# A two-layer decoder trunk in fp32: raw gate/up weights in six tiles instead of three, and weight preparation by 1,024 columns

## The chip, the core and the metric

The kernel runs on one core of one Trainium2 chip. The metric is the device time in microseconds. TensorE (PE) multiplies, VectorE (DVE), ScalarE (ACT) and GpSimd (POOL) do the elementwise work, and SyncE's queue (SP) issues every DMA of the kernel.

## What is computed

Sequence 1,024, width 1,024, two layers, each an attention and a SwiGLU mixer. Cut to what matters here:

```python
def swiglu(h, w_gate_up, w_down):
    gate, up = jnp.split(h @ w_gate_up, 2, axis=-1)     # 1024 -> 2 x 2816
    return (jax.nn.silu(gate) * up) @ w_down            # 2816 -> 1024
...
    for layer in range(DEPTH):
        h = rms_norm(x, mix_pre_g[layer])
        ...   # layer 0: differential attention; layer 1: stick-breaking attention with
        ...   # q = h @ b_w_q and k, v = rms_norm(x, kv_norm_g) @ kv_w
        x = x + rms_norm(m, mix_post_g[layer])
        f = swiglu(rms_norm(x, ffn_pre_g[layer]), ffn_w_gate_up[layer], ffn_w_down[layer])
        x = x + rms_norm(f, ffn_post_g[layer])
```

## The kernel before, in words

Every fp32 operand of a product is split into a high part (fp32r, a rounded copy) and a low part (what the rounding lost), and a product is three passes on PE: high by high, low by high, high by low. The two mixers' products are cut further into seven half-size products of sums and differences of blocks, in place of eight.

**The order of the work** is made when the kernel is built. `Weaver` (line 82) runs the kernel's parts as threads. A thread names the engine and the planned cost of its next step (`yield DVE(1024)`), takes tiles from pools (`yield acq(S_tr)`) and waits for events; of the ready steps of an engine the one with the lower priority number goes first. `InOrder` (line 277) records each instruction as it comes, so that every engine and SP's queue have one fixed order. On the chip the engines keep that order and wait for each other by semaphores; how long things take there doesn't change it.

**The gate/up stage** (`gate_up`, line 1735, once for each layer; mixer A at about 0.65 to 1.1 ms, mixer B at about 2.02 to 2.45 ms) runs over 22 blocks of 128 hidden columns. A block, called a quad below, is loaded by `loader` into two raw tiles (128x1024, the gate columns and the up columns), with a third raw tile as scratch. `quad` (line 510) makes seven operands from them: five need a sum or a difference on DVE; each is rounded by ACT into a `w` tile's first half, and the low part is subtracted by POOL (six of seven) or DVE (one). There are nine `w` tiles. The three raw tiles are given back when all seven operands of the quad are there. PE then does 7 x 12 = 84 matmuls of 512 columns for the quad (against `hT` or `hx`, the split activations), into one of eight PSUM banks for each operand; `take` (line 1785) adds each bank into four 128x512 tiles (named `e`) on DVE and ACT.

```python
S_raw = Slots(tiles(cpool, 3, [P, 1024], F32, "raw"))
S_tr = Slots(tiles(cpool, 5, [P, 1024], F32, "tr"))
```

For each pair of quads `pair_ops` (line 1747) forms the sums and differences that the down product needs and stores them to HBM (`op`); its three sums take a tile of the 12 scratch tiles `S_sg` or, where none is free, one of the five `tr` tiles. `tr` tiles are otherwise used where the stages change (transpositions, norms, `transition`).

**The preparation of the second attention's weights** (`pre_weights`, line 413) runs beside mixer A. For 24 blocks (b_w_q and kv_w, eight each of q, k, v; a job below) it loads 128x1024 values into a `tr` tile, multiplies by the norm's gain (a column for each of eight 128-column pieces), and stores the high part and the low part to HBM (`prebq`, `prebk`, `prebv`). Eight more jobs without a gain follow for b_w_o (`prewo`). ACT makes the high part by eight 128-column activations, DVE the low part by eight 128-column instructions.

**The down stage** of mixer A follows (about 1.1 to 1.36 ms, `down`), with operands made from `hT` on the same engines, and ends with `transition`, which uses `tr` tiles.

## Time and profile before

| | |
|---|---|
| median of 3 runs | 2686.43 us (2685.59 to 2689.43) |
| the profiled execution | 2685.22 us |
| its span, first to last instruction | 2683.4 us, so 1.8 us lie around it |
| mean granted TensorE clock | 0.977 of full |
| busy: PE, DVE, ACT, POOL | 2519.7, 2061.2, 1288.8, 806.8 us |
| raw gate/up loads | 88 of 512 KB, median 5.1 us from issue to landing |

An engine's busy time is a union of its instructions; a busy PE is not a PE at its peak, and a share over the whole span mixes stages with different limits. The useful views are therefore the table by stage, the waits of one stage, and the chain of work that ended last. In group rows "x144 | 79.4, 590" is the count, the busy us and the mean ns of one. A wait is put down to what came last.

### The profile page before, as it was taken

The numbers are of one execution on the slowest core, as the hardware profiler recorded it, in microseconds if no ns is written. First come the engines' busy times: TensorE is split into PE (matmuls) and PEld (weight loads), VectorE is DVE, ScalarE is ACT, GpSimd is POOL, SyncE is SP. The second block draws the span as 40 slices with busy tenths as digits, with TensorE's granted clock in tenths as the row PEclk, the third lists the DMA queues.
The fourth block names the chain that finished last, engine by engine and source line by source line (L and its number), as shares of the span: only waits on it lengthen the run. The fifth ranks groups of instructions, "written<-read, shape, count | busy, mean of one in ns | idle before, by whom it ended". The sixth has DMA issues, their size and how long they took to land.

```text
span 2683.4 us, 37281 instructions
## 1 busy us (share of the span) xinstructions
PE 2519.7 (94%) x12555; PEld 2117.6 (79%) x12555; DVE 2061.2 (77%) x3559; ACT 1288.8 (48%) x2926; POOL 806.8 (30%) x733
## 2 busy tenths in 40 slices
PE   8999999897999989899899999999989999999998
PEld 8998999775877777677678888888777877777887
DVE  4767676866887878689978888778777777676898
ACT  4555565644444444454246655556454333334532
POOL 2111112333343333435510000000033444445553
PEclk9999999998999999899999999999999999999999
DMA  6333333441566545665474444444543433337325
GB/s 172 82 79 79 91 81 103 120 165 67 171 210 203 198 145 174 234 208 180 170 243 109 112 113 113 120 117 130 199 153 110 130 129 127 98 102 239 110 83 177
DMA packets 286335, 378.78 MB, mean 141 GB/s; under 512 B 24448, under 2 KB 182528, under 8 KB 285568
## 3 DMA queue, kind: packets, MB, share of 16 engines
q1 hardware_dynamic: 286144, 376.40, 45.2%
q8 instruction: 99, 1.62, 0.3%
q14 instruction: 92, 0.75, 0.1%
HBM read 230.70 MB, written 114.16 MB: 129 GB/s over the span
## 4 chain that ended last, share of the span: by engine, by line
PE 42%; DVE 29%; DMA 11%; issue 7%; ACT 5%; POOL 4%; SPq 1%; DVEq 0%; ACTq 0%; POOLq 0%
PE bank L286 42%; DVE e L286 7%; DVE raw L286 7%; DVE tr L286 6%; DMA raw<-in_ffn_w_gate_up_dram 5%; POOL w L286 3%; ACT w L286 2%; DVE rB L286 2%; DMA tr<-in_kv_w_dram 2%; DVE atB L286 1%; DVE w L286 1%; SPq L286 1%; DVE fb L286 1%; ACT e L286 1%; DVE fa L286 1%
## 5 line engine op out<-in xcount | busy, mean ns | idle before, releaser
L286 PE MATMUL bank<-hT,w 128*128 128x512 f32 x3264 | 817.5, 402 | 49.9 <-POOL w L286 21.1
L286 POOL TENSOR_TENSOR w<-raw,w 128x512 fp32r<-128x512 f32 (+1 forms) x363 | 552.9, 1535 | 772.1 <-ACT w L286 698.6
L286 PEld LDWEIGHTS bank<-hT,w 128*128 128x128 f32 x3264 | 611.5, 192 | 192.9 <-POOL w L286 33.0
L286 ACT CAST w<-raw 128x512 fp32r<-128x512 f32 x398 | 244.6, 621 | 603.3 <-DVE raw L286 412.1
L286 PE MATMUL bank<-hx,w 128*128 128x512 f32 x1584 | 367.7, 389 | 4.7 <-DVE hx L286 4.7
L286 DVE TENSOR_TENSOR e<-e,bank 128x512 f32<-128x512 f32 x480 | 311.9, 676 | 68.5 <-ACT e L286 49.1
L286 PEld LDWEIGHTS bank<-hx,w 128*128 128x128 f32 x1584 | 296.9, 188 | 68.4 <-DVE hx L286 7.0
L286 PE MATMUL bank<-w,hT 128*128 128x384 f32 (+1 forms) x1728 | 344.9, 346 | 5.5 <-DMA w<-prewo 3.1
L286 PEld LDWEIGHTS bank<-w,hT 128*128 128x128 f32 x1728 | 300.2, 189 | 15.8 <-DMA w<-prewo 3.5
L286 PE MATMUL bank<-w,fb 128*128 128x512 f32 x1204 | 295.3, 395 | 14.2 <-DVE e L286 5.8
L286 PEld LDWEIGHTS bank<-w,fb 128*128 128x128 f32 x1204 | 227.8, 190 | 66.7 <-DVE fb L286 4.2
L286 DVE TENSOR_TENSOR raw<-raw 128x512 f32<-128x512 f32 x88 | 80.1, 930 | 159.6 <-DMA raw<-in_ffn_w_gate_up_dram 159.6
L286 PE MATMUL bank<-ident,tr 128*128 128x128 f32 x1059 | 161.4, 280 | 37.0 <-DVE tr L286 19.0
L286 PE MATMUL bank<-w,fa 128*128 128x512 f32 x692 | 181.7, 403 | 14.4 <-DVE e L286 4.5
L286 PEld LDWEIGHTS bank<-ident,tr 128*128 128x128 f32 x1059 | 128.0, 143 | 68.0 <-DVE tr L286 20.1
L286 POOL MEMSET atB<- 128x128 f32 x128 | 25.1, 205 | 498.3 <-PE bank L286 492.7
L286 PEld LDWEIGHTS bank<-w,fa 128*128 128x128 f32 x692 | 133.6, 194 | 47.6 <-POOL w L286 4.4
L286 POOL TENSOR_TENSOR sm<-sm,nhalf 128x1 f32<-128x1 f32 (+1 forms) x72 | 56.8, 790 | 299.3 <-DVE sm L286 296.7
L286 DVE TENSOR_TENSOR_SCAN rB<-rB,zeroB 128x512 f32<-128x512 f32 (+3 forms) x145 | 134.8, 947 | 6.0 <-ACT rB L286 5.6
L286 DVE TENSOR_TENSOR raw<-raw,raw 128x512 f32<-128x512 f32 x132 | 134.4, 1018 | 0.0
L286 ACT CAST atB<-bank 128x512 fp32r<-128x512 f32 (+1 forms) x160 | 84.5, 554 | 88.8 <-PE bank L286 82.7
L286 DVE TENSOR_TENSOR atB<-bank,atB 128x512 fp32r<-128x512 f32 (+1 forms) x160 | 97.6, 629 | 32.9 <-ACT atB L286 32.4
(224 smaller groups left out, 3854.5 us busy)
## 6 DMA issues: line engine op xcount, KB each, us to landing
raw<-in_ffn_w_gate_up_dram SPq DMA_DIRECT2D x88, 512.0 KB, 5.1
op<-e SPq DMA_DIRECT2D x99, 256.0 KB, 4.1
xy<-st SPq DMA_DIRECT2D x192, 128.0 KB, 2.3
xyB<-stB SPq DMA_DIRECT2D x176, 128.0 KB, 3.8
fb<-op SPq DMA_DIRECT2D x79, 256.0 KB, 3.5
wd<-in_ffn_w_down_dram SPq DMA_DIRECT2D x36, 512.0 KB, 6.2
hT<-wd SPq DMA_DIRECT2D x72, 256.0 KB, 5.4
raw<-in_a_w_qkv_dram SPq DMA_DIRECT2D x96, 128.0 KB, 2.6
```

What stands on the lines that cost most here:

```text
L286: return tc.keep_in_program_order(f(*a, **k))
```

## The change

Four things change, and the planner then builds a new order from them.

1. When all seven activation operands of a mixer are there, a thread `lend_raw` takes three of the five `tr` tiles and lends them to `loader` as raw tiles (`S_rx`) until the gate/up stage's end. `loader` takes raw tiles from both pools. It does so in both mixers.
2. The three sums of `pair_ops` take `S_sg` tiles only, and `pair_ops` gets priority -5 in place of 25 (A) and 46 (B).
3. `pre_weights` multiplies by the gain with one DVE instruction of 1,024 columns, rounds with one ACT instruction of 1,024 columns, and subtracts with one DVE instruction of 1,024 columns, instead of eight and eight of 128.
4. `pre_weights` waits for the seven activation operands instead of the phase's end and 25 us; its threads' priority is 40 in place of 60, and its planned pause between jobs 6.0 us in place of 13.5. With three `tr` tiles lent, two are left for it.

```diff
--- before.py
+++ after.py
@@ -335,7 +335,7 @@
     actd = {f: drp.tile([P, T], F32, name=f"act{f}") for f in range(ND, NF)}
     opd = [{i: drp.tile([P, 512], F32, name=f"op{p}_{i}") for i in DORD} for p in range(ND // 2)]
 
-    S_half, S_trx = Slots(), Slots()
+    S_half, S_trx, S_rx = Slots(), Slots(), Slots()
 
     def halves(t):
         return [t[:, :512], t[:, 512:]]
@@ -411,8 +411,8 @@
     pres = []
 
     def pre_weights(ready):
-        yield ready
-        yield delay(25.0)
+        for ev in ready:
+            yield ev
 
         def work(job, raw, hi):
             if job.gain is not None:
@@ -420,20 +420,11 @@
                 yield g_ev
             h = hi.t.bitcast(F32R)
             if job.gain is not None:
-                for c in range(NC):
-                    cs = slice(c * P, c * P + P)
-                    yield ACT(P, 1)
-                    act.activation(h[:, cs], raw.t[:, cs], AF.Copy, scale=g[:, c:c + 1])
-                for c in range(NC):
-                    cs = slice(c * P, c * P + P)
-                    yield DVE(P + 58)
-                    dve.scalar_tensor_tensor(raw.t[:, cs], raw.t[:, cs], g[:, c:c + 1], hi.t[:, cs],
-                                             op0=ALU.mult, op1=ALU.subtract)
-            else:
-                yield ACT(1024)
-                act.copy(h, raw.t)
+                v3 = raw.t.rearrange("p (c n) -> p c n", c=NC)
                 yield DVE(1024)
-                dve.tensor_tensor(raw.t, raw.t, hi.t, op=ALU.subtract)
+                dve.tensor_tensor(v3, v3, g.unsqueeze(2).broadcast_to([P, NC, P]), op=ALU.mult)
+            yield ACT(1024)
+            act.copy(h, raw.t)
 
             def store(x, cs):
                 yield SP(1.0)
@@ -442,8 +433,10 @@
                 W.put(x)
                 W.set(job.ev)
 
-            W.spawn(store(hi, slice(0, 1024)), 60, "prest")
-            W.spawn(store(raw, slice(1024, 2048)), 60, "prest")
+            yield DVE(1024)
+            dve.tensor_tensor(raw.t, raw.t, hi.t, op=ALU.subtract)
+            W.spawn(store(hi, slice(0, 1024)), 40, "prest")
+            W.spawn(store(raw, slice(1024, 2048)), 40, "prest")
 
         for job in pres:
             raw = yield acq(S_tr)
@@ -451,8 +444,8 @@
             yield SP(1.0)
             sp.dma_start(out=job.view(raw.t), in_=job.src)
             yield delay(2.6)
-            W.spawn(work(job, raw, hi), 60, "pre" + job.name)
-            yield delay(13.5)
+            W.spawn(work(job, raw, hi), 40, "pre" + job.name)
+            yield delay(6.0)
 
     def loader():
         queue = []
@@ -615,11 +608,11 @@
             if isinstance(job, QuadJob):
                 rr = []
                 for src in job.srcs:
-                    raw = yield acq(S_raw)
+                    raw = yield acq(S_raw, S_rx)
                     yield SP(1.0)
                     sp.dma_start(out=cview(raw.t)[0], in_=src.rearrange("(c p) n -> p c n", p=P))
                     rr.append(raw)
-                rr.append((yield acq(S_raw)))
+                rr.append((yield acq(S_raw, S_rx)))
                 yield delay(2.6)
                 W.spawn(quad(k, job, *rr), plan("p.splitg", 20), "quad" + job.name)
                 yield delay(-2.6)
@@ -1687,8 +1680,11 @@
             own = tiles(plG, 6, [P, 4, 512], F32R, "hx")
             W.spawn(hin.combine(own), -20, "combine")
             W.spawn(scratch(), -20, "scratch")
+            bookR = []
+            W.spawn(lend_raw(bookR), -20, "lendraw")
             W.set(opened)
             yield gu_done
+            W.unlend(bookR)
             gG.__exit__(None, None, None)
             g, pl = phase_pool("dn" + nm, "right")
             acc.extend(tiles(pl, 2, [P, D], F32, "acc"))
@@ -1710,6 +1706,11 @@
         W.spawn(opener(), -30, "open")
         W.spawn(hin.ready(), 0, "ready")
 
+        def lend_raw(book):
+            for i in MORD:
+                yield hin.op_ev[i]
+            yield from W.lend(S_tr, S_rx, 3, whole, book)
+
         def scratch():
             W.spawn(lend_q(), -20, "lendq")
             W.spawn(move_weights(), 60, "movew")
@@ -1752,7 +1753,7 @@
                 for i, x, k in ((3, a11, keep[0]), (4, a22, keep[1])):
                     W.spawn(store_op(p, i, x.t, k.done), pr, "storeo")
                 for i, x, y in ((2, a21, a22), (5, a11, a12), (1, a11, a22)):
-                    z = yield acq(S_sg, S_tr)
+                    z = yield acq(S_sg)
                     yield DVE(512)
                     dve.tensor_tensor(z.t[:, :512], x.t, y.t, op=ALU.add)
                     W.spawn(store_op(p, i, z.t[:, :512], lambda z=z: W.put(z)), pr, "storeo")
@@ -1819,7 +1820,7 @@
             for f in range(NF):
                 ss = []
                 if f < ND and f % 2 == 0:
-                    W.spawn(pair_ops(f // 2), plan("p.silu" + nm, 1), "pairo")
+                    W.spawn(pair_ops(f // 2), -5, "pairo")
                 job = st.q[f]
                 ev = {i: Ev() for i in MORD + ("s",)}
                 for i in MORD:
@@ -2331,7 +2332,7 @@
         W.spawn(wo_early("A", sA, eA), 75, "earlyMM")
         W.spawn(wo_early("B", sB, eB), 81, "earlyMM")
         W.spawn(phase_ffn("A", fA, "woA", hFA, xd[0], xd[1], ffn_post_g[0], hB), 26, "ffnA")
-        W.spawn(pre_weights(phase_done["woA"]), 60, "pre")
+        W.spawn(pre_weights([hFA.op_ev[i] for i in MORD]), 60, "pre")
         W.spawn(phase_B(), 1, "B")
         W.spawn(phase_wo("B", sB, "B", oB, xd[1], xd[2], mix_post_g[1], ffn_pre_g[1], hFB, eB), -5, "woB")
         W.spawn(load_early(eB, "B", oB, lambda m: [oB_ev[p][m // 2] for p in range(7)], sB), -41, "earlyB")
```

**SP's queue in mixer A's gate/up stage** (the whole of one quad period, from one quad's load to the next one's). Before, `raw` and `tr` tiles are apart, and each period has one job's load (here b_w_q) and the two stores of the job ahead of it:

```order
L286 DMA raw0_125<-in_ffn_w_gate_up_dram 128x8x128
L286 DMA raw2_127<-in_ffn_w_gate_up_dram 128x8x128
L286 DMA tr2_130<-in_b_w_q_dram 128x8x128
L286 DMA wd0_10_244<-in_ffn_w_down_dram 16x8192
L286 DMA prebv1_257<-tr4_132 128x1024
L286 DMA prebv1_257<-tr1_129 128x1024
L286 DMA wd0_11_245<-in_ffn_w_down_dram 16x8192
L286 DMA raw0_125<-in_ffn_w_gate_up_dram 128x8x128
L286 DMA raw2_127<-in_ffn_w_gate_up_dram 128x8x128
L286 DMA tr3_131<-in_kv_w_dram 128x8x128
L286 DMA prebq2_258<-tr0_128 128x1024
L286 DMA prebq2_258<-tr2_130 128x1024
```

Now the quads' loads go to `tr3`, `tr4` and to `raw0`, `raw2` by turns, and the jobs go through `tr0` and `tr1` alone; this period has two job loads, each of which overwrites the tile that the job ahead of it has just stored from:

```order
L286 DMA tr1_129<-in_kv_w_dram 128x8x128
L286 DMA tr3_131<-in_ffn_w_gate_up_dram 128x8x128
L286 DMA tr4_132<-in_ffn_w_gate_up_dram 128x8x128
L286 DMA prebk2_259<-tr0_128 128x1024
L286 DMA prebk2_259<-tr1_129 128x1024
L286 DMA wd0_10_244<-in_ffn_w_down_dram 16x8192
L286 DMA tr0_128<-in_kv_w_dram 128x8x128
L286 DMA prebv2_260<-tr1_129 128x1024
L286 DMA prebv2_260<-tr0_128 128x1024
L286 DMA wd0_11_245<-in_ffn_w_down_dram 16x8192
L286 DMA raw0_125<-in_ffn_w_gate_up_dram 128x8x128
L286 DMA raw2_127<-in_ffn_w_gate_up_dram 128x8x128
```

From the fourth quad's load to the last quad's load there are 18 such periods in both orders; before they held one job's load each, now 24 between them, and three b_w_o jobs follow before the down stage.

**DVE in the same stage**, where one job's work stands between the additions of PE's banks (`e<-e,bank`) and the quad's differences. Before:

```order
L286 SCALAR_TENSOR_TENSOR tr2_130<-tr2_130,gB_103,tr4_132 128x128
L286 TENSOR_TENSOR e0_5589<-e0_5589,bank1_134 128x512
L286 TENSOR_TENSOR raw0_125<-raw0_125,raw2_127 128x512
L286 TENSOR_TENSOR e1_5590<-e1_5590,bank1_134 128x512
L286 SCALAR_TENSOR_TENSOR tr2_130<-tr2_130,gB_103,tr4_132 128x128 x2
L286 TENSOR_TENSOR e1_5590<-e1_5590,bank4_137 128x512
L286 TENSOR_TENSOR raw0_125<-raw0_125,raw2_127 128x512
L286 SCALAR_TENSOR_TENSOR tr2_130<-tr2_130,gB_103,tr4_132 128x128 x3
L286 TENSOR_TENSOR e1_5590<-e1_5590,bank2_135 128x512
L286 SCALAR_TENSOR_TENSOR tr2_130<-tr2_130,gB_103,tr4_132 128x128 x2
```

Now (`tr0` is the job's raw tile, `tr1` its high part; `tr3` and `tr4` hold a quad):

```order
L286 TENSOR_TENSOR e0_5589<-e0_5589,bank1_134 128x512
L286 TENSOR_TENSOR tr3_131<-tr3_131,tr4_132 128x512
L286 TENSOR_TENSOR e1_5590<-e1_5590,bank1_134 128x512
L286 TENSOR_TENSOR tr0_128<-tr0_128,gB_103 128x1024
L286 TENSOR_TENSOR e1_5590<-e1_5590,bank4_137 128x512
L286 TENSOR_TENSOR tr3_131<-tr3_131,tr4_132 128x512
L286 TENSOR_TENSOR tr0_128<-tr0_128,tr1_129 128x1024
L286 TENSOR_TENSOR e0_5589<-e0_5589,bank2_135 128x512
```

Eight narrow instructions became two wide ones, the gain's product and the subtraction, with two other instructions between them. The product stands behind the job's load, the subtraction behind ACT's rounding.

**SP's stores of the pair sums in mixer B.** Before, three of the first pair's stores come from `tr` tiles:

```order
L286 DMA op0_3_173<-e2_16085 128x512
L286 DMA op0_4_174<-e1_16084 128x512
L286 DMA op0_2_171<-tr0_128 128x512
L286 DMA op0_5_172<-tr1_129 128x512
L286 DMA op0_1_177<-tr2_130 128x512
```

Now all come from `S_sg`'s `e` tiles:

```order
L286 DMA op0_3_173<-e2_15765 128x512
L286 DMA op0_4_174<-e1_15764 128x512
L286 DMA op0_2_171<-e2_15765 128x512
L286 DMA op0_5_172<-e2_15765 128x512
L286 DMA op0_1_177<-e1_15764 128x512
```

## Rows read from the trace of the kernel before

**Rows 1.** The page, part 1: busy us, share, instructions.

```profile
PE 2519.7 (94%) x12555; PEld 2117.6 (79%) x12555; DVE 2061.2 (77%) x3559; ACT 1288.8 (48%) x2926; POOL 806.8 (30%) x733
```

**Rows 2.** Stages: us, each engine's busy us (count), PEclk, DMA share, GB/s.

```profile
692.00:1088.70 396.70, 368.33 (x1553) 295.07 (x1552) 316.67 (x482) 175.09 (x382) 155.65 (x108) 0.97 0.55 183
1140.00:1200.00 60.00, 56.07 (x239) 45.83 (x240) 50.91 (x67) 37.86 (x78) 24.07 (x16) 0.97 0.59 197
1200.00:1250.00 50.00, 46.22 (x198) 36.35 (x197) 47.25 (x63) 22.11 (x42) 22.43 (x15) 1.00 0.64 214
1250.00:1300.00 50.00, 44.41 (x179) 35.10 (x177) 48.82 (x60) 18.65 (x32) 27.36 (x15) 0.93 0.45 151
1320.00:1360.00 40.00, 34.29 (x145) 26.73 (x144) 33.37 (x49) 13.11 (x26) 12.73 (x10) 0.91 0.53 190
2030.00:2454.00 424.00, 410.18 (x1777) 334.69 (x1777) 306.20 (x386) 156.74 (x282) 188.69 (x128) 0.99 0.40 130
2500.00:2560.00 60.00, 60.00 (x266) 49.67 (x266) 56.44 (x71) 25.58 (x45) 33.80 (x22) 1.00 0.37 110
```

**Rows 3.** Waits, 660 to 1110 us: us in total, times, longest.

```profile
DVE raw L286 <- DMA raw<-in_ffn_w_gate_up_dram: 60.0, 20, 4.4
```

**Rows 4.** Waits, 2030 to 2455 us.

```profile
DVE raw L286 <- DMA raw<-in_ffn_w_gate_up_dram: 92.0, 20, 6.1
```

**Rows 5.** Timeline of the second gate/up stage: start, us, engine, instruction, [idle before].

```profile
2237.14 1.01 SPq L286 DMA_DIRECT2D raw<-in_ffn_w_gate_up_dram  x2
...
2243.82 1.29 DVE L286 TENSOR_TENSOR raw<-raw 128x512 f32<-128x512 f32 x2 [5.56 <-DMA raw<-in_ffn_w_gate_up_dram]
...
2247.54 10.73 PE L286 MATMUL bank<-hT,w 128*128 128x512 f32 x46 [1.32 <-POOL w L286]
...
2257.05 1.00 SPq L286 DMA_DIRECT2D raw<-in_ffn_w_gate_up_dram  x2
```

**Rows 6.** The chain that ended last: start us, us, what.

```profile
692.13 5.27 DMA raw<-in_ffn_w_gate_up_dram
...
1088.68 6.14 DMA raw<-in_ffn_w_gate_up_dram
...
1320.85 6.37 DMA tr<-in_b_w_o_dram
```

**Rows 7.** Groups, DVE, 692 to 1088.7 us: busy us, mean ns, idle before.

```profile
L286 DVE SCALAR_TENSOR_TENSOR tr<-tr,gB,tr 128x128 f32<-128x128 f32 x144 | 79.4, 590 | 0.0
```

**Rows 8.** Groups, DVE, 1140 to 1320 us.

```profile
L286 DVE SCALAR_TENSOR_TENSOR tr<-tr,gB,tr 128x128 f32<-128x128 f32 x24 | 21.7, 948 | 0.0
```

**Rows 9.** Tile tr, 660 to 1350 us: ns min/median/max.

```profile
L286 ACT CAST tr<-tr x7: 1043/1046/1047, 1224.4 to 1344.7; 128x1024 fp32r<-128x1024 f32 x7
...
L286 DVE TENSOR_TENSOR tr<-tr,tr x7: 1209/1212/2315, 1235.5 to 1345.8; 128x1024 f32<-128x1024 f32 x7
```

**Rows 10.** Tensor kv_w: its loads' issue to landing.

```profile
DMA to landing us min/median/max: 4.7/6.8/7.4
```

**Rows 11.** Tensor prewo, 700 to 1350 us: its stores' issue to landing.

```profile
DMA to landing us min/median/max: 2.6/3.6/6.8
```

**Rows 12.** DMA issues, 700 to 1090 us: count, KB each, median us to landing.

```profile
raw<-in_ffn_w_gate_up_dram SPq DMA_DIRECT2D x36, 512.0 KB, 5.2
...
prebk<-tr SPq DMA_DIRECT2D x12, 512.0 KB, 6.8
```

**Rows 13.** DMA issues, 2040 to 2440 us.

```profile
op<-e SPq DMA_DIRECT2D x36, 256.0 KB, 4.3
...
op<-tr SPq DMA_DIRECT2D x27, 256.0 KB, 2.0
```

**Rows 14.** Timeline, DVE, at 903 and at 2248 us.

```profile
903.48 0.68 DVE L286 TENSOR_TENSOR raw<-raw,raw 128x512 f32<-128x512 f32 x1
...
2247.96 1.78 DVE L286 TENSOR_TENSOR raw<-raw,raw 128x512 f32<-128x512 f32 x1
```


## The prediction

> **What bounds the kernel now.** I read the page's first part, then the table by stage, then the waits and the timeline of the two gate/up stages, then the chain. PE is busy 94% of the span [rows 1], so a change can win only what PE loses in a stage, and busy time doesn't show that: the rate of matmuls does. Where PE has nothing to wait for it does 266 matmuls in 60.0 us at the full clock [rows 2], 0.2256 us each, so a quad's 84 take 18.95 us. Against that price, mixer B's gate/up stage has 1777 matmuls in 424.0 us, worth 400.9: **23.1 us lost**. Mixer A's, in the 396.7 us between its fourth quad's load and its last, has 1553, worth 350.4: **46.3 us lost**. In the down stage of A the three stretches from 1140 to 1300 hold 616 matmuls, worth 139.0 of 160 us: **21.0 us lost**. In the 40 us behind that, PE is idle for 5.7 us [rows 2].
>
> The cause in the two gate/up stages is one loop. DVE waits 20 times for a raw load in each, 60.0 us in A and 92.0 us in B [rows 3, 4]. The timeline shows a turn of it: a raw pair is issued at 2237.14, DVE gets it at 2243.82 after 5.56 us of idleness, PE waits 1.32 us for POOL's low part at 2247.54, and the next pair is issued at 2257.05, when the last operand of this quad is done [rows 5]. That is 19.9 us a turn with the load inside it; nothing is in flight while the operands are made. In A the turn is longer: from 692.13 to 1088.68 [rows 6] there are 18 pairs (36 loads [rows 12]), 22.0 us each, because DVE also has the weight jobs to do (144 narrow instructions, 79.4 us [rows 7]).
>
> **The change, part by part.**
>
> *Six raw tiles, mixer B.* The pair of the next quad can now land while this one is split, so the 6.7 us from issue to DVE's start [rows 5] leave the loop and some 13.2 us of making operands stay, less than PE's 18.95. DVE is busy 306.2 of 424.0 us [rows 2], which at PE's pace is under 80%. PE becomes the bound. The first three quads still go through three tiles, since lending waits for all seven activation operands. I take **-19 us**; bounds 0 and -23.
>
> *Six raw tiles, mixer A.* The same would give up to -46. But the price is paid from the `tr` pool: the weight jobs now go through two tiles, one job after the other. The order puts 24 job loads into the 18 periods in place of 18, so at PE's pace (18 x 18.95 = 341 us) a job may take 14.2 us. Its loop is: load, gain product, rounding, store of the high part, and then the next load, which overwrites that tile. No row shows the loop alone, so I bound it by its pieces. The load: 4.7 to 7.4 us, median 6.8 [rows 10]. The product: no such instruction is in the trace, the nearest is the 1,024-column subtraction, 1.21 us, at most 2.3; the rounding 1.05 [rows 9]. The store: 2.6 to 6.8 us [rows 11], 6.8 as the median of the present jobs' stores, which are issued in one burst with a raw pair and a load [rows 12]. The sum runs from 9.6 to 17.6 us. I take 6.2 + 1.4 + 1.05 + 4.8, since these transfers will more often be alone than now, and 1 us for four handovers and SP's issue: 14.5 us. 24 x 14.5 = 348 us, just above PE's 341. Two loops of nearly equal length that stand in the same in-order queues cost more than the longer one: when DVE waits for a job's load, the bank additions and the quad's differences behind it wait too (eight banks, 2.7 us of PE each, cover a single wait), and SP holds a quad's load behind a job's store (the quad ahead covers that). I add 5%, a guess, which makes 365 us, 20.3 us a quad, against 396.7: **-31 us**; bounds +25 (17.6 x 24 = 422) and -46.
>
> *The weight jobs' arithmetic.* ACT's eight instructions become one of 1.05 us, off the path. On DVE in A's gate/up stage 316.7 us of work in 18 periods is 17.6 a quad [rows 2], of which 4.4 are narrow instructions [rows 7]; the wide pair adds 24/18 x 2 x 1.21 = 3.2. That makes 16.4 of 18.95 us: room, but little. It enters the term above and isn't counted again.
>
> *Mixer A's down stage.* Three jobs with a gain (24 narrow instructions, 21.7 us of DVE [rows 8]) and three of eight b_w_o jobs leave it for the gate/up stage. DVE is busy 96 of the 100 us from 1200 to 1300 [rows 2], so its work does count here; but PE's losses there go to POOL's low parts and the operand loads as well. **-10 us**, bounds 0 and -21. At its end the chain runs through a b_w_o load of 6.37 us [rows 6]; the jobs now end sooner and the tiles are free: **-3 us**, bounds 0 and -6.
>
> *Sums in `S_sg` only, `pair_ops` early.* I cost these at nothing. The eight banks cover a late sum. A store from an `e` tile lands in 4.3 us where one from a `tr` tile took 2.0 [rows 13]; if the cover were gone, 2.3 us for each of 18 pairs would be 41 us. The early start of the jobs costs nothing either: their first load stands behind the fourth quad's instead of the third's. SP issues as many transfers as before.
>
> The sum is -19 - 31 - 10 - 3 = -63 us. The profiled execution took 2685.2 us (its span and 1.8 us), 1.2 below the median; 2686.4 - 63 gives **2623 us**.
>
> **The rivals.**
>
> *PE bounds everything* (16%). If the jobs' loop stays under 14 us, all losses go: -23 - 46 - 21 - 6 = -96, 2590 us. For it: the short ends of the load and store rows. Against it: the loop's middle is already at the limit, and DVE at 87%.
>
> *DVE bounds mixer A* (13%). The same kind of instruction takes 0.68 us in one place and 1.78 in another, while POOL subtracts [rows 14]; the wide one 1.21 or 2.3 [rows 9]. If both wide instructions of each job meet POOL, they cost 24/18 x 2 x 2.3 = 6.1 us a quad, DVE has 17.6 - 4.4 + 6.1 = 19.3 us to do, and with 5% for its waits A takes 365 us for the 18 periods; the down stage, where POOL is as busy, then gives nothing: -19 - 32 - 3 = -54, 2632 us. The Trainium skill (SBUF — State Buffer, section "SBUF: two separate sides") gives the rule: a DVE instruction with two SBUF inputs and a GpSimd one take a shared port pair as an exclusive lock for the whole instruction, and the later fully blocks. By that rule longer instructions block POOL longer, which speaks against the wide form; the two durations of one form agree with it.
>
> *The jobs' loop bounds mixer A* (12%). At 16.5 us a job, 24 take 396 us, what A takes now: A gives nothing, -19 - 10 - 3 = -32, 2654 us.
>
> *Slower* (6%). The same loop, longer: it decides from the point where 24 jobs eat all the other gains, (396.7 + 32) / 24 = 17.9 us. A load of 7.4, a product of 2.3, a store of 6.8 and 1 us of handovers make 18.6 with the rounding: 446 us, +49 - 32 = +17, 2703 us. Against it: the long stores of now come with their burst, and half of the jobs' stores would have to stay so.
>
> *It doesn't do what it says* (3%): the lent tiles hold no load early enough, nothing moves, 2686 us. The new order speaks against it: loads go to `tr3`, `tr4` and `raw0`, `raw2` by turns.
>
> **The numbers.** The forecast has 50%: near balance of PE and jobs in A, 2605 to 2645 us. The range 2585 to 2665 takes in the first three rivals and the down stage's bounds. A measurement of this kernel can tell about 0.2%, 5.4 us, from no change. The forecast and three rivals are faster, 91%; same 3%; slower 6%.
>
> **What would show it.** Right: DVE's waits for raw loads nearly gone in both stages; B's 1777 matmuls in about 405 us; A's 18 periods near 20 us with DVE or ACT waiting for b_w_q and kv_w loads in their place; 24 jobs done before the down stage; the wide subtraction at 1.2 to 2.3 us. Wrong: raw waits still there in B (then the loop wasn't the bound), a period in A at 22 us with each job near 16 (the jobs bind), or PE waiting for banks behind `pair_ops`.

## The result, and the profile after

The changed kernel takes **2615.93 us** (median of 4 runs, 2611.42 to 2617.21) against 2686.01 us before (4 runs, 2685.36 to 2689.43): ratio **0.9734**, 95% interval 0.9717 to 0.9750. The forecast was 2623 us, range 2585 to 2665.

The two profiled executions (2685.22 and 2614.90 us), cut where PE starts another kind of matmul (the first on `hx`, the first `w,fa` of the down stage, the first `hT,w` of the attention, the first and the last `hx` of mixer B):

| us | before | after | change | forecast |
|---|---|---|---|---|
| up to mixer A | 659.0 | 658.4 | -0.6 | 0 |
| A gate/up | 456.4 | 413.2 | **-43.2** | -31 |
| A down | 268.8 | 252.6 | **-16.2** | -10 and -3 |
| second attention | 637.1 | 644.6 | **+7.5** | 0 |
| B gate/up | 430.9 | 410.3 | **-20.6** | -19 |
| B down to the end | 231.2 | 234.0 | +2.8 | 0 |
| span | 2683.4 | 2613.1 | -70.3 | -63 |

Page of the changed kernel, part 1 (busy us, share, instructions), beside [rows 1]:

```profile
PE 2495.1 (95%) x12555; PEld 2111.9 (81%) x12555; DVE 2027.7 (78%) x3415; ACT 1265.5 (48%) x2758; POOL 805.0 (31%) x733
```

PE's share hardly moves. What PE loses shows in the table by stage (columns as in [rows 2]): A's gate/up from its first `hx` on, its 18 periods between the fourth quad's load and the last, three stretches of A's down stage, B's gate/up.

```profile
658.40:1071.50 413.10, 400.96 (x1759) 329.07 (x1757) 366.24 (x440) 185.33 (x309) 194.73 (x123) 1.00 0.67 222
669.40:1031.20 361.80, 359.43 (x1581) 296.43 (x1582) 320.64 (x390) 157.54 (x264) 172.37 (x109) 1.00 0.70 229
1140.00:1200.00 60.00, 60.00 (x266) 49.69 (x265) 58.69 (x69) 27.05 (x46) 31.72 (x20) 1.00 0.61 203
1200.00:1250.00 50.00, 45.33 (x193) 34.98 (x191) 50.00 (x63) 17.36 (x31) 26.91 (x16) 1.00 0.27 76
1978.00:2379.10 401.10, 400.82 (x1768) 331.93 (x1769) 283.77 (x383) 162.62 (x279) 170.38 (x128) 1.00 0.41 135
```

At the forecast's price of 0.2256 us a matmul, the 18 periods of A hold 1581 matmuls worth 356.7 us in 361.8: **5.1 us lost, where 46.3 were lost before** [rows 2]. B loses 2.2 us of 401.1 (1768 matmuls, 398.9). The granted clock is 1.00 in A, PE's upper level of 2.4 GHz throughout, where it was 0.97, a mean with some of the lower one, 1.2. The down stage still loses: from 1200 to 1250 DVE is busy all 50.00 us and PE has 193 matmuls, worth 43.5.

Over the whole of A's gate/up stage, whose matmuls are worth some 396 us, PE lost 60 us before and loses 17 now. The row of the kernel before for that stage (PE idle for 38.4 us, now for 12.1):

```profile
659.00:1115.40 456.40, 418.03 (x1757) 333.86 (x1755) 362.72 (x548) 207.23 (x448) 176.54 (x124) 0.97 0.54 178
```

The waits of DVE, first A's gate/up stage, then B's (in total, times, longest), beside [rows 3, 4]:

```profile
DVE tr L286 <- DMA tr<-in_kv_w_dram: 15.0, 9, 3.0
...
DVE tr L286 <- DMA tr<-in_b_w_q_dram: 9.3, 5, 3.6
...
DVE raw L286 <- DMA raw<-in_ffn_w_gate_up_dram: 2.3, 1, 2.3
...
DVE raw L286 <- DMA raw<-in_ffn_w_gate_up_dram: 2.1, 1, 2.1
```

60.0 and 92.0 us of waits for raw loads have become 2.3 and 2.1. In A, waits for the weight jobs' loads stand in their place, 24.3 us, and PE hardly feels them. PE's longest waits in A's stage:

```profile
PE bank L286 <- ACT w L286: 7.0, 1, 7.0
PE bank L286 <- DVE hx L286: 3.1, 3, 1.2
```

The 7.0 us are one wait, at the stage's end, for the first operand of the down stage. The weight jobs have a part in it: the down stage's first loads (`hT<-wd`) stand in SP's queue right behind the two stores of a job (`prewo`), which wait for the job's rounding and subtraction, and are issued 5.1 us before PE's first matmul of the down stage, at 1071.56 (timeline of SP):

```profile
1064.56 1.82 SPq L286 DMA_DIRECT2D prewo<-tr  x2
1066.47 5.38 SPq L286 DMA_DIRECT2D hT<-wd  x10
```

Where no job's store stands just ahead of them, as with one tile lent or with the narrow form (below), they are issued 12.9 and 8.4 us before that matmul, and PE waits for 0.9 and 0.3 us. That order wasn't changed by itself.

A turn of the loop in B (timeline), beside [rows 5]:

```profile
2187.16 1.00 SPq L286 DMA_DIRECT2D raw<-in_ffn_w_gate_up_dram  x2
...
2206.10 1.20 DVE L286 TENSOR_TENSOR raw<-raw 128x512 f32<-128x512 f32 x1
2206.78 1.01 SPq L286 DMA_DIRECT2D tr<-in_ffn_w_gate_up_dram  x2
...
2208.01 11.04 PE L286 MATMUL bank<-hT,w 128*128 128x512 f32 x48
```

The pair issued at 2187.16 is first touched at 2206.10, with no idle time ahead of it; the next goes into lent `tr` tiles. It was 6.7 us from issue to use before, all inside the turn; it is now 18.9, all beside other work.

The jobs' new instructions in A, on DVE (ns min/median/max), beside [rows 7, 9]:

```profile
L286 DVE TENSOR_TENSOR tr<-tr,tr x62: 677/1212/2326, 683.1 to 1174.7; 128x1024 f32<-128x1024 f32 x32, 128x512 f32<-128x512 f32 x30
L286 DVE TENSOR_TENSOR tr<-tr,gB x24: 1211/1226/2319, 680.8 to 1030.5; 128x1024 f32<-128x1024 f32 x24
```

### The profile page after: what moved, and what is told of

Same layout as the page of the kernel before. It is cut to its first block, busy times and chain, and to the rows that moved or that the text cites. A ratio compares the mean times of both kernels' runs of the same rounds, so it can differ in the third digit from the quotient of the medians.

```text
span 2613.1 us, 37165 instructions
## 1 busy us (share of the span) xinstructions
PE 2495.1 (95%) x12555; PEld 2111.9 (81%) x12555; DVE 2027.7 (78%) x3415; ACT 1265.5 (48%) x2758; POOL 805.0 (31%) x733
## 5 line engine op out<-in xcount | busy, mean ns | idle before, releaser
L286 PE MATMUL bank<-hT,w 128*128 128x512 f32 x3264 | 801.8, 395 | 5.6 <-DMA w<-prebq 2.9
L286 PEld LDWEIGHTS bank<-hT,w 128*128 128x128 f32 x3264 | 603.2, 189 | 126.7 <-DMA w<-prebq 2.5
L286 POOL TENSOR_TENSOR w<-raw,w 128x512 fp32r<-128x512 f32 (+1 forms) x243 | 374.6, 1553 | 460.6 <-ACT w L286 406.9
L286 ACT CAST w<-raw 128x512 fp32r<-128x512 f32 x258 | 158.9, 623 | 318.0 <-DVE raw L286 280.9
L286 POOL TENSOR_TENSOR w<-tr,w 128x512 fp32r<-128x512 f32 x120 | 176.6, 1483 | 229.7 <-ACT w L286 201.2
L286 PEld LDWEIGHTS bank<-ident,tr 128*128 128x128 f32 x1059 | 130.2, 145 | 67.4 <-DVE tr L286 21.5
L286 ACT CAST w<-tr 128x512 fp32r<-128x512 f32 x140 | 85.9, 620 | 164.2 <-DVE tr L286 156.2
L286 DVE TENSOR_TENSOR e<-e,e 128x512 f32<-128x512 f32 x124 | 125.1, 1033 | 7.1 <-ACT e L286 6.4
L286 ACT COPY e<-bank 128x512 f32<-128x512 f32 x168 | 93.9, 588 | 68.0 <-PE bank L286 68.0
```

The lines of the kernel that those rows point to most:

```text
L286: return tc.keep_in_program_order(f(*a, **k))
```

## The experiments

Four theories were put to the test. Theory 1, the prediction's: the reload wait of a raw pool of three tiles is the loss of both gate/up stages, and the lent tiles win it back. Theory 2: A's gain is that of the wide instructions, a lighter DVE. Theory 3: the down stage's gain is that of jobs that end ahead of it. And, for the second attention, that the jobs' new start or the sums' new rule lengthened it.

Stages are cut as above. What matters in A is two numbers that trade against each other: how many of the 32 weight jobs have had their load issued when the down stage begins, and the lengths of the two stages. The stage lengths come from one profiled execution of each kernel. Four of the kernels (lent in B alone, one lent, two lent, before + start and pace) have the same order of PE's, DVE's and ACT's instructions in the second attention, buffer numbers left aside, and took 642.0 to 647.1 us there; so a difference of up to some 5 us in one stage, between two kernels, may be no more than that.

| kernel | us (median) | ratio to before, 95% | A gate/up | jobs ahead of down | A down | attention | B gate/up |
|---|---|---|---|---|---|---|---|
| before | 2686.0 | 1 | 456.4 | 21 | 268.8 | 637.1 | 430.9 |
| the change | 2615.9 | 0.9717 to 0.9750 | 413.2 | 27 | 252.6 | 644.6 | 410.3 |
| lent in B alone | 2644.3 | 0.9799 to 0.9846 | 454.6 | 32 | 244.5 | 645.0 | 409.3 |
| lent in A alone | 2632.1 | 0.9758 to 0.9815 | 412.2 | 27 | 251.5 | 643.2 | 429.4 |
| one lent in A | 2632.4 | 0.9773 to 0.9802 | 439.7 | 32 | 247.1 | 647.1 | 409.3 |
| **two lent in A** | **2605.8** | **0.9674 to 0.9703** | 413.8 | 31 | 249.2 | 643.6 | 409.2 |
| two lent, pace 3.0 | 2606.8 | 0.9682 to 0.9711 | 412.5 | 31 | 249.0 | 643.6 | 409.7 |
| narrow form | 2628.6 | 0.9734 to 0.9788 | 402.5 | 18 | 277.9 | 647.2 | 410.3 |
| two lent, narrow form | 2638.8 | 0.9795 to 0.9828 | 430.4 | 20 | 270.3 | 643.3 | 409.3 |
| before + wide form | 2692.4 | 1.0000 to 1.0026 | 466.6 | 21 | 265.1 | 637.0 | 433.4 |
| old start and pace | 2622.7 | 0.9730 to 0.9775 | 417.9 | 21 | 262.3 | 640.0 | 410.0 |
| before + start and pace | 2657.8 | 0.9873 to 0.9916 | 444.3 | 32 | 247.4 | 642.0 | 430.0 |
| sums' old rule | 2617.2 | 0.9716 to 0.9745 | 415.3 | 28 | 253.9 | 647.7 | 410.2 |
| stores twice | 2639.7 | 0.9801 to 0.9834 | 433.9 | 27 | 255.7 | 644.7 | 410.4 |

### Lending in one mixer alone

In `lend_raw`:

```diff
-            yield from W.lend(S_tr, S_rx, 3, whole, book)
+            if nm == "B":
+                yield from W.lend(S_tr, S_rx, 3, whole, book)
```

> The change with the lending of three tr tiles kept in mixer B alone; mixer A's gate/up stage has three raw tiles and five tr tiles, the wide weight instructions and the new start and pace of the weight jobs. Theory 1 (the reload wait of a three-tile raw pool is the loss of both gate/up stages): A's gate/up stage (413 us changed, 456 before) gets longer than in the change by 20 to 43 us, B's stays near 410 us, the whole 2635 to 2660 us. Rival theory 2 (A's gain comes from wide weight instructions, a lighter DVE): A's stage stays within 8 us of 413 us and the whole is near 2616 us. Theory 3 (the jobs' earlier end brings the down stage's 16 us): the down stage stays near 253 us here, as the jobs keep their early start.

A's gate/up stage goes back to 454.6 us, near the top of theory 1's range (433 to 456); theory 2 falls. DVE's waits in that stage (this kernel) are nearly those of [rows 3] again, and PE waits for operands, 32.5 us:

```profile
DVE raw L286 <- DMA raw<-in_ffn_w_gate_up_dram: 53.9, 19, 5.3
...
PE bank L286 <- POOL w L286: 16.5, 13, 2.0
PE bank L286 <- ACT w L286: 16.0, 10, 4.2
```

But the down stage, where I expected 253 us, takes 244.5: with all five `tr` tiles the jobs turn every 13.7 us and all 32 are through before it. Lending in A wins 41.4 us of gate/up and gives 8.1 back in the down stage.

The mirror image, `if nm == "A":` in the same place:

> The change with the lending kept in mixer A alone; mixer B's gate/up stage has three raw tiles as before. Theory 1: B's gate/up stage returns from 410 to about 431 us, A's stays near 413 us, the whole is 2616 + 20 = 2636 us. Rival (B's gain comes from the sums that now go through S_sg alone, or from the early start of the pair's sums, which this kernel keeps): B's stage stays near 410 us and the whole near 2616 us.

B returns to 429.4 us, and its waits for raw loads (this kernel, B's gate/up) to those of [rows 4]:

```profile
DVE raw L286 <- DMA raw<-in_ffn_w_gate_up_dram: 93.2, 20, 5.8
```

The whole, 2632.1, is 4 us under what I expected, the stage 1.6 us under. The rival falls: with the sums' new rule, which this kernel keeps, B is as long as before, within 1.5 us. In all fourteen kernels PE does B's matmuls in the same order; with the lending B takes 409.2 to 410.4 us, without it 429.4 to 433.4.

### How many tiles

```diff
-            yield from W.lend(S_tr, S_rx, 3, whole, book)
+            yield from W.lend(S_tr, S_rx, 2 if nm == "A" else 3, whole, book)
```

> The change with two tr tiles lent in mixer A in place of three (five raw tiles, three for the weight jobs); mixer B lends three. Theory 1: with five raw tiles a pair can still land while the other is split, so A's gate/up stage stays within 5 us of 413 us; the jobs' loop through three tiles no longer binds at all, so if the jobs' loop was what kept A over PE's price (theory 1b) the stage shortens by 3 to 10 us, and the whole is 2604 to 2616 us. Rival (three pairs must be in hand, since the third raw tile of a turn is freed last): A's stage grows by 10 to 20 us and the whole to 2626 to 2636 us.

Theory 1 holds: five raw tiles do as well as six (413.8 us). The gain came elsewhere than theory 1b put it: gate/up doesn't shorten, for PE sets it already, but through three `tr` tiles the jobs turn every 12.9 us in place of 14.9, so 31 are through in place of 27, and the down stage is 3.4 us shorter. That is a third of the 9.9 us between the two profiled spans; 4.5 lie in the last stage (234.0 to 229.5 us), where not the edit but the planner's new order counts (below), and the rest are pieces of about 1 us. **This version beats both kernels**: its interval, 0.9674 to 0.9703, lies below the change's.

With `1 if nm == "A"`:

> The change with one tr tile lent in mixer A (four raw tiles, four for the weight jobs). With five raw tiles A's stage was no longer than with six. A turn holds two loads and a third tile until its last operand is done, so with four tiles one of the next two loads can run beside the split and the other waits: I expect a third to a half of the reload loss back, A's gate/up stage at 425 to 440 us and the whole at 2620 to 2632 us, with DVE waits for raw loads again. Rival: one load ahead is enough (the second lands while the first is split); then the stage stays within 5 us of 413 and the whole is 2600 to 2612 us.

It came out at the top of the range, 439.7 and 2632.4 us. With four raw tiles some 26 of the 41 us are lost again, nearly two thirds, where I had expected a third to a half: DVE waits 25.0 us for raw pairs and PE 13.0 us for POOL's low parts (this kernel, 660 to 1090 us).

```profile
DVE raw L286 <- DMA raw<-in_ffn_w_gate_up_dram: 19.1, 10, 3.8
...
DVE raw L286 <- DMA tr<-in_ffn_w_gate_up_dram: 5.9, 3, 2.2
...
PE bank L286 <- POOL w L286: 13.0, 10, 2.0
```

Two lent, and the jobs' pace (`yield delay(6.0)` to `3.0`):

> Two tr tiles lent in mixer A and the pace between job loads cut from 6.0 to 3.0 us. With two lent and the old pace 31 of the 32 jobs had their load before the down stage. If each job moved out of the down stage saves about 2.3 us there, this one more saves 2 us at most: the whole 2602 to 2607 us. Rival: a denser burst of loads and stores stands in SP's queue before the raw pairs and PE loses 5 us or more in the gate/up stage: 2610 us or more.

No difference, 2606.8 us; again 31 jobs ahead of the down stage. The pace no longer decides.

### The form of the jobs' arithmetic

Eight ACT roundings with the gain and eight DVE instructions of 128 columns put back into the change:

```diff
-                v3 = raw.t.rearrange("p (c n) -> p c n", c=NC)
-                yield DVE(1024)
-                dve.tensor_tensor(v3, v3, g.unsqueeze(2).broadcast_to([P, NC, P]), op=ALU.mult)
-            yield ACT(1024)
-            act.copy(h, raw.t)
+                for c in range(NC):
+                    cs = slice(c * P, c * P + P)
+                    yield ACT(P, 1)
+                    act.activation(h[:, cs], raw.t[:, cs], AF.Copy, scale=g[:, c:c + 1])
+                for c in range(NC):
+                    cs = slice(c * P, c * P + P)
+                    yield DVE(P + 58)
+                    dve.scalar_tensor_tensor(raw.t[:, cs], raw.t[:, cs], g[:, c:c + 1], hi.t[:, cs],
+                                             op0=ALU.mult, op1=ALU.subtract)
...
```

> The change with the weight jobs' old arithmetic: eight ACT roundings and eight DVE instructions of 128 columns for each job with a gain; lending, start and pace are the change's. A job's loop gets no longer by a product on DVE (the rounding reads the raw tile with the gain), but DVE's work per quad in A grows by about 24/18 x (8 x 0.55 - 2.4) = 2.7 us, from 17.8 to 20.4 us, over PE's 18.95. Theory 2 (the wide instructions are needed): A's gate/up stage grows by 15 to 30 us over 413 us, the whole to 2630 to 2645 us. Theory 1 (six tiles do it, the form hardly matters): A's stage within 8 us of 413 us, the whole 2612 to 2624 us.

Both were wrong about the place. A's gate/up is *shorter*, 402.5 us: it holds 18 jobs in place of 27, one every 22.1 us, and the nine others lengthen the down stage by 25.3 us. Of the 10.7 us that gate/up gains, the wait at its end makes 6.7 (0.3 us in place of 7.0), and in the 18 periods 1.8 us are lost in place of 5.1. The two stages together are 14.6 us longer; the whole is 12.7 in the medians and 7 by the ratios, whose intervals overlap. Here the order was planned anew with the narrow costs, so this is the narrow form and the order it leads to.

The wide form alone, in the kernel before (the stores' threads keep the change's priority of 40 with it):

> The kernel before with the wide weight instructions alone (gain product, rounding and subtraction by 1,024 columns), nothing lent, old start and pace of the jobs. Theory 1: A's loop of a raw load in series with the operands stays, so only DVE's lighter work inside that loop counts: A's gate/up stage shorter by 0 to 10 us, down stage by 0 to 8 us, B's gate/up unchanged, the whole 2670 to 2686 us. Theory 2: A's gate/up stage shorter by 20 us or more, the whole below 2665 us.

Theory 2 fell here too, and theory 1's sign was wrong for gate/up: 10.2 us *longer*, with 3.7 us back in the down stage, and the whole, 2692.4, is above its range. DVE's waits for raw loads rise from 60.0 to 90.5 us, but its waits for ACT's additions fall from 31.5 to 1.9, so the sum of the two hardly moves. Of the 10.2 us, 3.8 are idle time of PE (42.2 us in place of 38.4); the rest is busy time, at a granted clock of 0.95 in place of 0.97. The wide product costs 2.00 us, its mean in the change being 1.48 (this kernel, A's gate/up: waits, the stage, the group):

```profile
DVE raw L286 <- DMA raw<-in_ffn_w_gate_up_dram: 90.5, 20, 6.2
```

```profile
657.30:1123.90 466.60, 424.43 (x1760) 340.35 (x1759) 358.65 (x430) 180.35 (x305) 201.26 (x124) 0.95 0.54 178
```

```profile
L286 DVE TENSOR_TENSOR tr<-tr,gB 128x1024 f32<-128x1024 f32 x21 | 42.1, 2003 | 12.0 <-DMA tr<-in_kv_w_dram 8.2 <-DMA tr<-in_b_w_q_dram 3.8
```

The narrow form once more, with one more `tr` tile left to the jobs:

> Two tr tiles lent in mixer A, three in B, and the weight jobs' old narrow instructions; start and pace are the change's. With one tr tile fewer for the jobs and the narrow form only 18 jobs had gone through before the down stage, with the wide form 27. With nothing lent the wide form made A's gate/up stage 10 us longer at the same pace (455 us against 444), and 10 us longer at the old pace (467 against 456). If the wide form is needed only because two tiles are few, the narrow jobs here turn in about 13 to 15 us through three tiles, 27 or more are through before the down stage, and the whole is within 6 us of 2606 us. Rival: the narrow form loads DVE past PE's price whatever the tiles, jobs slip into the down stage again (fewer than 24 before it) and the whole is 2615 us or more.

The edit is that of the narrow form, with two tiles lent in A. The rival's numbers held: 20 jobs ahead of down, one every 21.5 us, 2638.8 us, 33 more than with the wide form. Its reason, DVE loaded past PE's price, didn't: DVE is busy for 363.6 of the stage's 430.7 us. DVE's narrow instructions, PE's waits and DVE's longest in A's gate/up (this kernel):

```profile
L286 DVE SCALAR_TENSOR_TENSOR tr<-tr,gB,tr 128x128 f32<-128x128 f32 x152 | 95.2, 645 | 0.0
```

```profile
PE bank L286 <- DVE e L286: 11.5, 7, 7.1
```

```profile
DVE e L286 <- ACT e L286: 59.6, 25, 7.5
```

So in A's two stages together the wide form, with the order that is planned from it, wins 14.6 us with three tiles lent and 37.7 with two (700.7 against 663.0), and where nothing is lent it costs 10 us of gate/up, at the old pace (466.6 against 456.4) as at the new (454.6 against 444.3, two kernels that differ in the sums' rule as well). The narrow jobs aren't slow by themselves: with five `tr` tiles (below) they turned every 12.6 us. Why they turn at 21.5 through three tiles isn't settled; DVE's total doesn't tell, but DVE waits 59.6 us there for ACT's share of the additions, where with the wide form and two tiles lent it was 8.9.

### Start and pace

The change with the old start (25 us behind the output projection), the old priority 60 (the stores' threads keep 40) and the old pace:

```diff
-            yield delay(6.0)
+            yield delay(13.5)
...
-        W.spawn(pre_weights([hFA.op_ev[i] for i in MORD]), 60, "pre")
+        W.spawn(pre_weights(phase_done["woA"]), 60, "pre")
```

> The change with the weight jobs' old start (25 us behind the end of the output projection), old priority and old pace of 13.5 us; lending, wide instructions and the sums are the change's. Theory 3 (the down stage's 16 us come from jobs that end sooner): at the old pace jobs are left for the down stage, which returns to 262 to 270 us from 253, while A's gate/up stage stays within 5 us of 413 us; the whole 2622 to 2632 us. Theory 1 alone: both stages stay, 2612 to 2620 us. On the second attention, which every kernel with the change's start and pace took in 643 to 647 us where before it took 637: if start and pace re-plan it, it returns to 637 us here.

As theory 3 had it: 21 jobs ahead, and the down stage back at 262.3 us. The second attention took 640.0 us, between the two values named. The other half, the new start, pace and priority (these lines the other way round) in the kernel before, with nothing else of the change:

> The kernel before with the change's start, pace and priority of the weight jobs alone: nothing lent, the old narrow instructions, the old sums. Theory 3 (the down stage is shortened by jobs that end ahead of it, some 2.3 us a job): more than 21 of the 32 jobs have their load before A's down stage, which falls from 269 to 244 to 255 us, while A's gate/up stage, with three raw tiles and more narrow work on DVE, stays at 450 to 465 us; the whole 2665 to 2690 us. Rival: the down stage's gain needs the lending or the wide form, and it stays at 262 us or more. On the second attention: if start and pace of the jobs are what lengthens it, it takes 643 to 648 us here in place of 637; if it is the lending, it stays at 637.

All 32 jobs are through ahead of the down stage, at 12.6 us each, and it takes 247.4 us. What I had not expected: gate/up, with its three raw tiles, is 12.1 us shorter as well, and so the whole, 2657.8, is below the range (the profiled execution, 2651.75, is the fastest of the four, so its stages may look some us too short). DVE waits less for raw loads there (this kernel; 60.0 before):

```profile
DVE raw L286 <- DMA raw<-in_ffn_w_gate_up_dram: 37.9, 14, 4.9
```

These lines alone make the kernel 1.05% faster (0.84 to 1.27%), some 28 us, about as much as lending in A brings when the rest is there (2644.3 to 2615.9; 24 us by the ratios).

### The sums, and the jobs' loop

```diff
-                    z = yield acq(S_sg)
+                    z = yield acq(S_sg, S_tr)
...
-                    W.spawn(pair_ops(f // 2), -5, "pairo")
+                    W.spawn(pair_ops(f // 2), plan("p.silu" + nm, 1), "pairo")
```

> The change with the activation sums' old rule: scratch or tr tiles, at the old planned priority. My costing is nothing: the whole within 5 us of 2616 us. Rival: the sums that borrow tr tiles take them from the raw pool and the jobs (one of five tiles for 2 to 4 us in each of 18 pairs), so both gate/up stages grow by 5 to 15 us each and the whole to 2626 to 2646 us. If the sums re-plan the second attention, it returns from 644 to 637 us here.

2617.2 us, 1.3 from the change: costed at nothing, and nothing it is. Nor do the sums lengthen the second attention: it takes 647.7 us here.

Every store of a job issued twice, first to a spare tensor:

```diff
+                sp.dma_start(out=job.d2[:, cs], in_=x.t)
                 sp.dma_start(out=job.d[:, cs], in_=x.t)
```

> The change with every store of a weight job issued twice, first to a spare DRAM tensor, with no change to the computation. It lengthens the real loop of a job (load, product, rounding, store, next load into the same tile) by about a half of what two stores take, 2 to 5 us, and SP's queue by some 2 us a job, while the order of the instructions stays. If the jobs' loop of 15 us was the balance point with PE (the prediction's term, 24 jobs in 18 periods), 27 jobs at 17 to 20 us each need 460 to 540 us and A's gate/up stage grows by 40 us or more. Rival: the 15 us between loads are set by PE's pace and the order, and the loop itself is shorter; then the stage grows by less than 15 us, with longer waits of DVE for the jobs' loads.

Between the two: A's gate/up grows by 20.7 us. Of these, 15.7 lie in the 18 periods (377.4 us, counted as above), 0.65 us for each of their 24 jobs, and 4.7 in the one wait at the stage's end, 11.7 us in place of 7.0. The second store lands in 5.0 to 5.5 us where the single one took 3.0 to 4.5 (medians), and stands behind the first's issue of about 0.4; so each job's loop got some 2 us longer (an estimate from these rows), of which about 1.3 were slack. The waits for raw loads stay at 2.2 us, so it isn't the quads' loads that the added traffic holds up. DVE's waits for kv_w loads rise from 15.0 to 26.1 us (this kernel, 660 to 1100 us):

```profile
DVE tr L286 <- DMA tr<-in_kv_w_dram: 26.1, 14, 5.4
```

The jobs' loop was near the balance point, then, but on the right side of it.

## Why the prediction was right, and where its terms were off

The sum, -63 against -70.3, is nearer than its terms. A's two stages gave 15.4 us more than forecast, and the second attention and the last stage took 10.3 us back that no term had; that the two nearly cancel is luck.

**B's gate/up, -19: measured -20.6.** The step holds in every part: raw waits gone, PE at its price (401.1 us for 1768 matmuls; the forecast had 405 for 1777), and undone by taking the lent tiles away.

**A's gate/up, -31: measured -43.2.** The mechanism was right, a size was off. The mis-sized step is "I add 5%, a guess, which makes 365 us": 17 us for two loops of nearly equal length in the same queues. The 365 us came out at 361.8, but with 28 more matmuls in them, worth 6.3 us: the loss in the 18 periods fell from 46.3 to 5.1, by 41.2 where the term had 31, and the other 2 us lie at the stage's edges, which the term left out. The pieces of the jobs' loop were estimated well: 5.8 us for a kv_w load (6.2), 1.48 for the product (1.4), 3.0 to 4.5 for a store (4.8). The jobs' loads come every 14.9 us (mean of 27 from 672.60 us on), but that isn't the loop's own length, which the forecast put at 14.5: by the doubled stores about 1.3 us of it are slack, so the loop takes some 13.6 us, an estimate. The collisions cost PE almost nothing: DVE's 14 waits for job loads, 24.3 us, are 3.6 us at most, and only 5.1 us are lost in the 18 periods, which fits the cover of the eight banks. "SP holds a quad's load behind a job's store (the quad ahead covers that)" is right inside the stage; at its end the job's stores stand ahead of the down stage's loads, nothing covers them, and PE waits 7.0 us. "PE bounds everything" asked for a loop under 14 us and was right for B and for A's 18 periods, and wrong for the end of A's gate/up stage and for the down stage.

**A's down stage, -10 and -3: measured -16.2.** Six more jobs went ahead of it, as counted (27 against 21). The price of a job was right, and another share was left out. The changed kernel with the old start and pace has the old 21 jobs ahead and a down stage of 262.3 us: 6.5 us of the 16.2 are there without the six jobs, and the wide form alone gave 3.7. The other 9.7, 1.6 us a job, are those of the six jobs, as the -10 had it, as far as one execution of each kernel tells. Over all kernels a job moved out of the stage is worth some 2.2 us with the narrow instructions (277.9 us with 18 ahead, 247.4 with 32) and 1.6 with the wide ones (262.3 to 265.1 with 21 ahead, 244.5 to 247.1 with 32). The -3 at the stage's end came too: PE's waits behind that `b_w_o` load (4.4 us from 1325 to 1331 in the kernel before) are 1.2 us in the changed kernel. But they are 0.8 with 21 jobs ahead as well, so it isn't the jobs' earlier end that took them away. DVE remains the limit in a part of the stage (50.00 of the 50 us from 1200 on), and the loss isn't gone.

**"The early start of the jobs costs nothing either".** This step failed, in both directions. With the new pace and priority it is worth some 28 us by itself (about 12 of them in gate/up, which no term had, since I took the raw loop's turn in A as fixed by its load and its operands). And it goes with a longer second attention: 637.1 and 637.0 us with the old start and nothing lent, 640.0 with the old start in the changed kernel, 642.0 to 647.7 in all eleven with the new one. In the three with the old start PE does that stage's instructions in one and the same order, in the eleven with the new start in others: the stage is planned anew. The loss is in pieces. From the kernel before to the changed one PE's idle time there grows from 18.7 to 22.6 us and its busy time by 3.5, at a granted clock of 0.98 in place of 0.99 (second attention, before and after):

```profile
1384.20:2021.30 637.10, 618.41 (x3457) 513.22 (x3457) 500.51 (x804) 362.06 (x810) 57.90 (x163) 0.99 0.46 135
1324.20:1968.70 644.50, 621.93 (x3456) 514.43 (x3457) 502.20 (x802) 362.07 (x808) 58.34 (x163) 0.98 0.45 130
```

Which instructions lose the time isn't settled.

**The sums, 0: measured within 1.3 us of it.** **The last stage, 0: measured +2.8.** No edit is made to B's down stage and what follows, but the order there is planned anew too. PE's order is the same in all fourteen kernels; ACT's is one in eleven of them, which took 229.5 to 231.6 us (231.2 before), and another in the change, in the kernel with lending in A alone and in the one with the stores twice, which took 234.0 to 234.7. In the change PE waits there once for ACT, 4.0 us; before it was 1.7.

**The rivals.** *DVE bounds A* fell: DVE is busy 320.6 of 361.8 us and PE keeps its price. The mechanism behind it is in the rows all the same: the wide product takes 1.21 us at best and 2.32 at most, 1.48 in the mean here and 2.00 in the kernel before with the wide form alone. In the changed kernel nine of the 24 products run while POOL does nothing, and take 1.22 to 1.23 us; fifteen run beside a POOL instruction, and all nine that take over 1.3 us are among them. With the wide form alone 22 of 24 run beside one. The Trainium skill (SBUF — State Buffer, section "SBUF: two separate sides") says that a DVE instruction with two SBUF inputs and a GpSimd one that reads SBUF exclude each other for their whole length. These lengths agree with it. The 10 us that the wide form costs alone may be the price of such waits, but no run here separates it from the new order and the lower clock. *The jobs' loop* as bound, and *slower* by the same loop, fell by some 1.3 us a job.

## What to carry to other kernels

A loop whose loads can't run ahead shows itself by the rate of the bounding engine in that stage against its rate where it waits for nothing; the busy share (94% and 95% here) hides it. One more pair of buffers was enough (one more buffer was not), and the next tile is worth more to the work that it was taken from: lend the smallest number that puts a whole turn's loads ahead. Side work with slack in its own loop costs the main engine little beside a stage that PE bounds (5.1 us lost in 361.8), but look at the stage's end, where its stores can stand ahead of the next stage's loads. Moved there out of a stage in which DVE is the limit it paid 1.6 to 2.2 us a job here, so count how many jobs are through, not only how long a stage is. And where an edit makes the planner build a new order, compare the orders of the stages that it doesn't touch before putting a difference down to the edit.

## What the runs showed of the hardware

Stores of 512 KB landed faster where they no longer stood in one burst: those of kv_w's high and low parts for k took 6.8 us in the median in the kernel before, issued in a burst with a raw pair and a load [rows 12], and 3.8 in the changed kernel (DMA issues, 660 to 1090 us; the spreading as the cause wasn't tried by itself):

```profile
tr<-in_kv_w_dram SPq DMA_DIRECT2D x16, 512.0 KB, 5.8
...
prebk<-tr SPq DMA_DIRECT2D x16, 512.0 KB, 3.8
```

The loss of a wait is not only the wait: of the 43.2 us that A's gate/up stage gave, 26.3 were idle time of PE (38.4 us before, 12.1 after); the rest was busy time, at a granted clock of 0.97 with PE waiting for each reload and 1.00 without. Where the down stage begins, behind the 7.0 us of idle time, the clock is lower again, 0.91 in this stretch of the changed kernel:

```profile
1072.00:1140.00 68.00, 63.43 (x253) 50.38 (x253) 39.66 (x48) 35.34 (x65) 31.97 (x23) 0.91 0.77 264
```
